# Query blocks of the differential heads from last to first, operands loaded by parts, and the gate's sigmoid by way of tanh

## The chip, the cores and the metric

The kernel runs on one core of one Trainium2 chip. The metric is device time in microseconds (us) of one execution. Five engines work side by side, each through its own instructions in order: TensorE (PE, matmuls and transposes; PEld is its weight load), VectorE (DVE), ScalarE (ACT), GpSimd (POOL) and SyncE (SP). SP does no arithmetic here; it issues most of the transfers (DMAs), POOL and ACT issue some. PSUM holds what matmuls write, in banks of 512 float32 a partition; SBUF holds the rest.

## The reference, cut to what matters

One decoder layer on 512 tokens of 2048 float32. A combined projection feeds four heads of gated linear attention (GLA) and four heads of differential softmax attention; their outputs side by side go through an output projection, and a gated MLP with a short convolution follows. The parts that the change touches:

```python
# differential attention, per head, causal, 4 blocks of 128 queries
s = einsum('bqhcd,bkhcd->bhcqk', qi, k) * scale + bias      # two score maps (c = 0, 1)
p = softmax(where(dist >= 0, s, -inf))
a = p[:, :, 0] - lam * p[:, :, 1]
o = einsum('bhqk,bkhe->bqhe', a, v)                          # then rmsnorm over the head
# gate of the GLA heads
gate = silu(gg)                                              # gg * sigmoid(gg)
o_a = rmsnorm(o_a, gla_norm) * gate
```

Query block qb sees keys 0 to 128 (qb + 1), so block 3 is four times as wide as block 0.

## The kernel before

Matrix products of the projections take float32 operands split in a high and a low part: `granule` (lines 128 to 140) copies a loaded `raw` tile with ACT into the high part (L137) and subtracts with DVE for the low part (L138), both into one of three slots of a tile called `ring`; three matmuls per pair of tiles then sum the products. `ring` is one tile of 7168 columns; the slots use at most its first 6896.

The token mixer's projection runs in ten units of 512 columns (`InUnit`, L727), each of which does seven block products instead of eight by sums of blocks (x0, z0, y0, z1, x1, y1, y2). Their weights are loaded with `load` (L102, on SP); some are added to a tile already there by POOL's accumulating DMAs (L751). Units 2, 3, 4 make the values and the operands of differential heads 0 and 1, units 5, 6, 7 those of heads 2 and 3, units 8 and 9 (`gate_unit`, L841) the gate. Results go to DRAM tiles (`dqd`, `dkd`: queries and keys of a head, already turned; `dvd`: values of two heads) and are fetched from there.

Beside the units runs a filler: the generators `gla_heads` and, after it, `diff_heads` (L617). `step` (L84) advances it, at a pace of 0.75 steps for each granule of a unit, 1.0 in the last unit. `diff_heads` is a pipeline over 16 blocks n (4 heads of 4 blocks). Step i calls, in this order, `store(i - 5)`, `values(i - 3)`, `probs(i)` and `turn(i - 2)`:

- `probs` (L637): two score maps (L645), bias, maximum, Exp (L653), sum, and the difference of the two maps;
- `turn` (L664): transposes of the block's probabilities, copied out by ACT as `aT` (L670);
- `values` (L673): the product of `aT` with the values (L677), then the norm, with its power on POOL;
- `store` (L686): two transposes (L690), a copy, and a DMA to `dstd` on ACT's queue (L693).

The queries and keys of a head fill four tiles of 128 x 512 under the tag `qk`, which has four buffers; the values fill one tile of 128 x 4 x 256 under the tag `v`, which has one. So the next head's queries and keys go where the last ones lay, and a load waits until these were read. `fetch(h + 1)` is called in the step of a head's last block, if the projection of head h + 1 is already traced (`there["diff"]`). Otherwise the next head's first step waits for it, fetches, and lets two more steps pass (two `yield`). `fetch_v(h)` is called in step 2 of head h, behind the `values` of the last block of head h - 1.

The gate (`done` in `gate_unit`) takes the unit's result u and the head's output op from DRAM: `op = op * u` (L850), `u = sigmoid(u)` on ACT (L851), `u = u * op` (L852). `turn_gate` (L870) and `place_diff` (L877) then lay the two groups' outputs out as the operand of the output projection.

Outside the blocks marked `manual_schedule`, where the written order holds, a planner orders the instructions of each engine: the order of tracing is the priority, and an instruction goes when a simulated timeline says that its operands and its buffer are ready. The differential heads and the gate are in the planned part. Dependences go by the part of a tile that is read or written.

Of the kernel before, what the change touches and what calls it, by code (L numbers as in the profile page):

```python
# [17 lines left out]
P = 128  # L18
D = 2048
S = 512  # L20
NT = S // P
# [4 lines left out]
DH, DQK, DDV = 4, 128, 256  # L26
# [9 lines left out]
def hybrid_layer(ctx: ExitStack, tc: tile.TileContext, x, attn_pre_norm, w_in, w_alpha_up, b_alpha,  # L36
# [10 lines left out]
    def dma(o, i):  # L47
        return nc.sync.dma_start(out=o, in_=i)
# [58 lines left out]
    RS = GR + P  # L107
    place_w = [LEVEL]

    ring = wpool.tile([P, 7 * GR], F32R, name="ring", bufs=1)  # L110
    slot = [0]

    def halves():
        slot[0] = (slot[0] + 1) % 3
# [218 lines left out]
    def qk_tile(name):  # L333
        return mx.tile([P, S], F32, name=name, tag="qk", bufs=4)
# [140 lines left out]
    there = {"gla": 0, "diff": 0}  # L475
# [141 lines left out]
    def diff_heads():  # L617
        dist = mx.tile([P, S], F32, name="dist", tag="md", bufs=1)
        nc.gpsimd.iota(dist, [[-1, S]], base=S - P, channel_multiplier=1, allow_small_or_imprecise_dtypes=True)
        nc.gpsimd.affine_select(dist, dist, [[-1, S]], ALU.is_ge, 1e34, base=S - P, channel_multiplier=1)  # L620
        dnb = mx.tile([P, DDV], F32, name="dnb", tag="nb", bufs=1)
        bcast_row(dnb, diff_norm[0])
        ts(dnb, dnb, 1.0 - LAMBDA_INIT, None, ALU.mult)
        qs, ks, vs = {}, {}, {}

        def fetch(h):
            qs[h], ks[h] = ([qk_tile(n) for _ in range(2)] for n in ("dq", "dk"))
            for i in range(2):
                dma(qs[h][i], dqd[h][:, i, :])
                dma(ks[h][i], dkd[h][:, i, :])  # L630

        def fetch_v(h):
            vs[h] = mx.tile([P, NT, DDV], F32, name="dvt", tag="v", bufs=1)
            e0 = (h % 2) * DDV
            dma(vs[h], dvd[h // 2][:, :, e0:e0 + DDV])

        def probs(n):  # L637
            h, qb = divmod(n, NT)
            q, k = qs[h], ks[h]
            slope = 2.0 ** (-8.0 * (h + 1) / DH)  # L640
            nk = (qb + 1) * P
            ps, ls = [], []
            for c in range(2):
                sb = bank()
                mm(sb[:, :nk], q[c][:, qb * P:(qb + 1) * P], k[c][:, :nk], start=True, stop=True)  # L645
# [7 lines left out]
                act(s[:, :nk], s[:, :nk], AF.Exp, bias=nm, scale=SC, accum_out=l)  # L653
# [7 lines left out]
            stt(ps[0][:, :nk], ps[0][:, :nk], ls[0], ps[1][:, :nk], ALU.mult, ALU.subtract)  # L661
            return ps[0]

        def turn(n, p):  # L664
            nk = (n % NT + 1) * P
# [4 lines left out]
            act(aT[:, :nk], tb[:, :nk], AF.Copy)  # L670
            return aT

        def values(n, aT):  # L673
            h, qb = divmod(n, NT)
            po = bank()
            for j in range(qb + 1):
                mm(po[:, :DDV], aT[:, j * P:(j + 1) * P], vs[h][:, j, :], start=j == 0, stop=j == qb)  # L677
            ss = small.tile([P, 1], F32, name="ss", tag="ss")
            jk = row_tile("jk")
            act(jk, po[:, :DDV], AF.Square, accum_out=ss)  # L680
            r = rsqrt_mean(ss, DDV)
            on = row_tile("on")
            stt(on, po[:, :DDV], r, dnb, ALU.mult, ALU.mult)
            return on

        def store(n, on):  # L686
            h, qb = divmod(n, NT)
            ob = bank(psm)
            for j in range(2):
                nc.tensor.transpose(ob[:, j * P:(j + 1) * P], on[:, j * P:(j + 1) * P], ident)  # L690
            o = row_tile("dst")
            act(o, ob[:, :2 * P], AF.Copy)
            nc.scalar.dma_start(out=dstd[h][:, :, qb * P:(qb + 1) * P], in_=o.rearrange("p (j c) -> p j c", j=2))  # L693

        N = DH * NT
        scored, turned, summed = {}, {}, {}
        fetch_v(0)
        for i in range(N + 5):
            h = i // NT
            if i < N and i % NT == 0:  # L700
                while there["diff"] <= h:
                    yield
# [138 lines left out]
    def gate_unit(c):  # L841
        heads = {}

        def before(j, i):
            op = heads[j, i] = tmp("op")
            dma(two(op), oad[2 * c + j][:, 2 * i:2 * i + 2, :])

        def done(j, i, u):
            op = heads.pop((j, i))
            tt(op, op, u, ALU.mult)  # L850
            act(u, u, AF.Sigmoid)  # L851
            tt(u, u, op, ALU.mult)  # L852
# [674 lines left out]
    u = ups[-1]  # L1527
# [161 lines left out]
```

## Time and profile before

| | |
|---|---|
| median of 3 runs | 2096.99 us (2095.53 to 2105.64) |
| profiled execution | 2102.56 us, its span 2100.9 us |
| PE busy | 2058.0 us, 98% of the span |
| DVE, ACT, POOL busy | 1504.4, 1001.0 and 286.3 us |
| HBM read and written | 311.72 and 44.56 MB, 170 GB/s over the span |
| differential heads on PE | first scores 386.28 us, last transposes 586.77 us |

The span runs from the first to the last recorded event; the execution's own time is 1.66 us longer. A row of the waits names an engine and line, what it waited for, then the total in us, the number of times and the longest. A row of the timeline has the start in us, the duration in us, the engine, the line, the operation, output and inputs, and in brackets the idle time before it with its releaser. A line number can be that of a helper: L48 is every plain DMA on SP, L102 every weight load.

### The profile page before, as it was taken

What the parts mean: (1) busy time and instruction counts of PE and PEld (TensorE: products, weight loads), DVE (VectorE), ACT (ScalarE), POOL (GpSimd) and SP (SyncE); (2) the same over time, 40 slices, a digit from 0 to 9 for tenths busy, and PEclk for the clock granted to TensorE, in tenths of its full rate; (3) what the DMA queues carried; (4) which work ended last, traced back from release to release, by engine and by line L of the source; (5) the groups of instructions that cost most, each with busy time, mean ns of one, the idle gap of its engine ahead of it and who ended that gap; (6) DMA issues with size and microseconds to landing.
All of it is one profiled execution on the core that took longest, in us unless ns stands there. A gap on an engine that the chain in (4) does not pass through costs nothing.

```text
span 2100.9 us, 35487 instructions
## 1 busy us (share of the span) xinstructions
PE 2058.0 (98%) x14417; PEld 1896.8 (90%) x14417; DVE 1504.4 (72%) x1790; ACT 1001.0 (48%) x1306; POOL 286.3 (14%) x306
## 2 busy tenths in 40 slices
PE   7999999999999999999999999999999999999997
PEld 6699999899988889899999999999999878887786
DVE  5967777666662255986777777777777778888877
ACT  5544444555652233454554554455455554444443
POOL 0112223222200000011111011111111110110100
PEclk9999999999999999999999999999999999999999
DMA  5488887878884244547668577567676876776763
GB/s 210 119 186 184 189 200 174 188 161 195 198 213 169 92 153 158 141 104 193 151 143 197 143 166 186 136 164 173 157 162 184 235 215 166 191 190 160 175 166 141
DMA packets 280698, 358.61 MB, mean 171 GB/s; under 512 B 14593, under 2 KB 221877, under 8 KB 278613
## 3 DMA queue, kind: packets, MB, share of 16 engines
q1 hardware_dynamic: 191380, 259.85, 36.9%
q0 software_dynamic: 84800, 94.38, 29.7%
q10 hardware_dynamic: 4352, 2.10, 0.4%
q8 instruction: 113, 1.85, 0.3%
q14 instruction: 53, 0.43, 0.1%
HBM read 311.72 MB, written 44.56 MB: 170 GB/s over the span
## 4 chain that ended last, share of the span: by engine, by line
PE 38%; issue 28%; DMA 2%; POOL 2%; DVE 1%; ACT 1%; POOLq 0%; DVEq 0%; SPq 0%; ACTq 0%
PE bank L1278 8%; PE bank L1279 8%; PE bank L1280 8%; PE bank L193 3%; PE bank L191 3%; PE bank L192 3%; POOL rt L1226 1%; PE bank L1381 1%; PE bank L1382 1%; POOL raw L1226 1%; PE bank L1380 1%; DMA raw<-in_w_ffn_in_dram 1%; DMA raw<-in_w_in_dram 1%; PE bank L1585 1%; PE bank L1586 1%
## 5 line engine op out<-in xcount | busy, mean ns | idle before, releaser
L138 DVE TENSOR_TENSOR ring<-raw,ring 128x1024 fp32r<-128x1024 f32 x315 | 383.5, 1223 | 277.9 <-ACT ring L137 277.1
L137 ACT ACTIVATE ring<-raw 128x1024 fp32r<-128x1024 f32 x315 | 333.3, 1060 | 520.9 <-PE bank L1279 112.4
L1280 PE MATMUL bank<-ah,ring 128*128 128x256 f32 x1280 | 353.4, 276 | 0.4 <-DVE ring L138 0.4
L1278 PE MATMUL bank<-ah,ring 128*128 128x256 f32 x1280 | 353.3, 276 | 0.0
L1279 PE MATMUL bank<-al,ring 128*128 128x256 f32 x1280 | 353.3, 276 | 0.0
L137 ACT ACTIVATE ring<-rt 128x1024 fp32r<-128x1024 f32 x221 | 233.1, 1060 | 241.2 <-PE bank L1279 147.9
L138 DVE TENSOR_TENSOR ring<-rt,ring 128x1024 fp32r<-128x1024 f32 x221 | 269.0, 1222 | 87.0 <-ACT ring L137 86.9
L1280 PEld LDWEIGHTS bank<-ah,ring 128*128 128x128 f32 x1280 | 240.3, 188 | 0.6 <-DVE ring L138 0.6
L1279 PEld LDWEIGHTS bank<-al,ring 128*128 128x128 f32 x1280 | 240.3, 188 | 0.1
L1278 PEld LDWEIGHTS bank<-ah,ring 128*128 128x128 f32 x1280 | 240.3, 188 | 0.1
L1381 PE MATMUL bank<-ring,ah 128*128 128x512 f32 x424 | 166.3, 392 | 5.3 <-DVE ring L138 5.3
L1382 PE MATMUL bank<-ring,al 128*128 128x512 f32 x424 | 165.2, 390 | 0.0
L1380 PE MATMUL bank<-ring,ah 128*128 128x512 f32 x424 | 158.8, 391 | 1.0 <-ACT ring L137 0.8
L192 PE MATMUL bank<-ring,ah 128*128 128x512 f32 x280 | 110.3, 395 | 0.9 <-DVE ring L138 0.9
L191 PE MATMUL bank<-ring,ah 128*128 128x512 f32 x280 | 109.9, 398 | 0.0
L193 PE MATMUL bank<-ring,al 128*128 128x512 f32 x280 | 109.7, 395 | 0.0
L1226 POOL DMA_DIRECT2D raw<-in_w_ffn_in_dram x40 | 51.2, 1308 | 398.1 <-DVE ring L138 398.1
L1381 PEld LDWEIGHTS bank<-ring,ah 128*128 128x128 f32 x424 | 79.6, 188 | 25.6 <-DVE ring L138 9.2
L1380 PEld LDWEIGHTS bank<-ring,ah 128*128 128x128 f32 x424 | 79.3, 188 | 19.9 <-ACT ring L137 3.4
L1226 POOL DMA_DIRECT2D rt<-in_w_ffn_in_dram x40 | 51.0, 1281 | 325.2 <-DVE ring L138 291.2
L777 PE MATMUL bank<-ring,ah 128*128 128x256 f32 x320 | 92.4, 289 | 2.6 <-ACT ring L137 1.3
L1382 PEld LDWEIGHTS bank<-ring,al 128*128 128x128 f32 x424 | 79.6, 188 | 16.3
(358 smaller groups left out, 5654.7 us busy)
## 6 DMA issues: line engine op xcount, KB each, us to landing
raw<-in_w_ffn_in_dram SPq DMA_DIRECT2D x96, 512.0 KB, 4.9
raw<-in_w_in_dram SPq DMA_DIRECT2D x56, 512.0 KB, 4.7
raw<-in_w_ffn_out_dram SPq DMA_DIRECT2D x48, 512.0 KB, 6.7
raw<-in_w_in_dram POOLq DMA_DIRECT2D x40, 512.0 KB, 7.1
rt<-in_w_ffn_in_dram SPq DMA_DIRECT2D x40, 512.0 KB, 5.7
rt<-in_w_ffn_in_dram POOLq DMA_DIRECT2D x40, 512.0 KB, 6.2
raw<-in_w_ffn_in_dram POOLq DMA_DIRECT2D x40, 512.0 KB, 6.8
raw<-in_w_o_dram SPq DMA_DIRECT2D x32, 512.0 KB, 4.0
```

Source lines behind the costliest of these rows:

```text
L137: act(hi, raw, AF.Copy)
L138: tt(lo, raw, hi.bitcast(F32), ALU.subtract)
L191: mm(banks[t], ah[:, t, s, :], w[0][:, k, :], start=st, stop=False)
L192: mm(banks[t], ah[:, t, s, :], w[1][:, k, :], start=False, stop=False)
L193: mm(banks[t], al[:, t, s, :], w[0][:, k, :], start=False, stop=sp)
L1226: nc.gpsimd.dma_start(out=raws[g].rearrange("p (a b) -> p a b", a=self.a), in_=self.block(0, j, g), accum_op=ALU.add)
L1278: mm(o, wh, sh[:, :, kk, :], start=start and kk == 0 and n == 0, stop=False, **NOW)
L1279: mm(o, wh, sl[:, :, kk, :], start=False, stop=False, **NOW)
L1280: mm(o, wl, sh[:, :, kk, :], start=False, stop=kk == HK - 1, **NOW)
L1380: mm(b[j], sh[:, o:o + P], w[0][:, q, :], start=start and st == 0, stop=False, **NOW)
L1381: mm(b[j], sh[:, o:o + P], w[1][:, q, :], start=False, stop=False, **NOW)
L1382: mm(b[j], sl[:, o:o + P], w[0][:, q, :], start=False, stop=st == 3, **NOW)
```

## The change

Three things are done.

Block n of head h is now block 3 - n of its queries (`place_of`), so each head begins with its widest block and ends with its narrowest.

Queries, keys and values of all heads use tiles that are made once. `fetch(h, lo, hi)` loads columns 128 lo to 128 hi of the four tiles. Behind the scores of block r = 2 the columns 256 to 511 of head h + 1 are fetched, if its projection is traced by then, and behind r = 3 the rest. Otherwise the head is fetched whole at its first step, which then lets three steps pass instead of two. The values are loaded in four parts, two of them in step 1 and two in step 2 of each head, behind the `values` of that step (all four at the start for head 0); part 0 of an odd head goes to 256 columns at the end of `ring` that no slot uses.

The gate uses sigmoid(u) = (1 + tanh(u / 2)) / 2: 0.5 op u, then tanh(0.5 u), then (tanh + 1) times the product.

```diff
     ring = wpool.tile([P, 7 * GR], F32R, name="ring", bufs=1)
+    ring_end = ring[:, 6 * RS:6 * RS + 256].bitcast(F32)
...
-        qs, ks, vs = {}, {}, {}
-        def fetch(h):
-            qs[h], ks[h] = ([qk_tile(n) for _ in range(2)] for n in ("dq", "dk"))
+        q, k = ([qk_tile(n) for _ in range(2)] for n in ("dq", "dk"))
+        vt = mx.tile([P, NT, DDV], F32, name="dvt", tag="v", bufs=1)
+
+        def value_tile(h, j):
+            return ring_end if j == 0 and h % 2 else vt[:, j, :]
+
+        def fetch(h, lo, hi):
+            sl = slice(lo * P, hi * P)
             for i in range(2):
-                dma(qs[h][i], dqd[h][:, i, :])
-                dma(ks[h][i], dkd[h][:, i, :])
-        def fetch_v(h):
-            vs[h] = mx.tile([P, NT, DDV], F32, name="dvt", tag="v", bufs=1)
+                dma(q[i][:, sl], dqd[h][:, i, sl])
+                dma(k[i][:, sl], dkd[h][:, i, sl])
+
+        def fetch_v(h, *js):
             e0 = (h % 2) * DDV
-            dma(vs[h], dvd[h // 2][:, :, e0:e0 + DDV])
+            for j in js:
+                dma(value_tile(h, j), dvd[h // 2][:, j, e0:e0 + DDV])
+
+        def place_of(n):
+            h, r = divmod(n, NT)
+            return h, NT - 1 - r
...
-        fetch_v(0)
+        got = set()
+
+        def ahead(h, r):
+            if r == 2 and h + 1 < there["diff"]:
+                fetch(h + 1, 2, 4)
+                got.add(h + 1)
+            elif r == 3 and h + 1 in got:
+                fetch(h + 1, 0, 2)
+
+        fetch_v(0, 3, 2, 1, 0)
...
-                if h not in qs:
-                    fetch(h)
+                if h not in got:
+                    fetch(h, 0, 4)
+                    got.add(h)
+                    yield
                     yield
                     yield
...
             if i - 3 in turned:
                 summed[i - 3] = values(i - 3, turned.pop(i - 3))
-            if i % NT == 2 and i > NT and h < DH:
-                fetch_v(h)
+                if i % NT == 1 and h < DH:
+                    fetch_v(h, 3, 2)
+                elif i % NT == 2 and h < DH:
+                    fetch_v(h, 1, 0)
             if i < N:
                 scored[i] = probs(i)
-                if i % NT == 3 and h + 1 < there["diff"]:
-                    fetch(h + 1)
+                ahead(h, i % NT)
...
-            tt(op, op, u, ALU.mult)
-            act(u, u, AF.Sigmoid)
-            tt(u, u, op, ALU.mult)
+            stt(op, op, 0.5, u, ALU.mult, ALU.mult)
+            act(u, u, AF.Tanh, scale=0.5)
+            stt(u, u, 1.0, op, ALU.add, ALU.mult)
```

More of the change, by code (lines that the diff above doesn't have):

```diff
@@ L623, in diff_heads @@
         ts(dnb, dnb, 1.0 - LAMBDA_INIT, None, ALU.mult)
-        qs, ks, vs = {}, {}, {}
-        def fetch(h):
-            qs[h], ks[h] = ([qk_tile(n) for _ in range(2)] for n in ("dq", "dk"))
+        q, k = ([qk_tile(n) for _ in range(2)] for n in ("dq", "dk"))
[4 more added lines that the diff above has]
+            sl = slice(lo * P, hi * P)
             for i in range(2):
-                dma(qs[h][i], dqd[h][:, i, :])
-                dma(ks[h][i], dkd[h][:, i, :])
-        def fetch_v(h):
-            vs[h] = mx.tile([P, NT, DDV], F32, name="dvt", tag="v", bufs=1)
+                dma(q[i][:, sl], dqd[h][:, i, sl])
+                dma(k[i][:, sl], dkd[h][:, i, sl])
+        def fetch_v(h, *js):
             e0 = (h % 2) * DDV
-            dma(vs[h], dvd[h // 2][:, :, e0:e0 + DDV])
+            for j in js:
[3 more added lines that the diff above has]
+            return h, NT - 1 - r
         def probs(n):
-            h, qb = divmod(n, NT)
-            q, k = qs[h], ks[h]
+            h, qb = place_of(n)
             slope = 2.0 ** (-8.0 * (h + 1) / DH)
@@ L664, in turn @@
         def turn(n, p):
-            nk = (n % NT + 1) * P
+            nk = (place_of(n)[1] + 1) * P
             tb = bank()
@@ L673, in values @@
         def values(n, aT):
-            h, qb = divmod(n, NT)
+            h, qb = place_of(n)
             po = bank()
             for j in range(qb + 1):
-                mm(po[:, :DDV], aT[:, j * P:(j + 1) * P], vs[h][:, j, :], start=j == 0, stop=j == qb)
+                mm(po[:, :DDV], aT[:, j * P:(j + 1) * P], value_tile(h, j), start=j == 0, stop=j == qb)
             ss = small.tile([P, 1], F32, name="ss", tag="ss")
@@ L686, in store @@
         def store(n, on):
-            h, qb = divmod(n, NT)
+            h, qb = place_of(n)
             ob = bank(psm)
```

## The prediction

> **What bounds the kernel now.** I read the page first, then the stretch that the edit touches: the differential heads and the two gate units, 367 to 660 us.
>
> ```profile
> span 2100.9 us, 35487 instructions
> PE 2058.0 (98%) x14417; PEld 1896.8 (90%) x14417; DVE 1504.4 (72%) x1790; ACT 1001.0 (48%) x1306; POOL 286.3 (14%) x306
> ```
>
> TensorE (PE) is busy for 98% of the span. The edit adds and removes no matmul, so what it can give is idle time of PE. The next view cuts the stretch into windows (length, busy time of PE, PEld, DVE, ACT and POOL, granted clock, DMA share, GB/s).
>
> ```profile
> 367.00:420.00 53.00, 49.74 (x383) 47.42 (x383) 34.87 (x76) 26.91 (x55) 11.18 (x14) 0.97 0.80 187
> ...
> 525.00:551.00 26.00, 24.49 (x197) 23.87 (x196) 14.97 (x26) 14.01 (x23) 5.10 (x6) 1.00 1.02 230
> ...
> 577.00:603.00 26.00, 24.64 (x206) 24.03 (x204) 11.27 (x13) 11.99 (x19) 5.36 (x7) 1.00 0.99 228
> 603.00:630.00 27.00, 24.11 (x154) 21.46 (x155) 22.45 (x31) 16.21 (x26) 0.00 (x0) 1.00 0.63 192
> ```
>
> PE idles 3.26, 1.51, 1.36 and 2.89 us in these four. The waits of PE between 330 and 660 us say for whom (total, times, longest):
>
> ```profile
> PE bank L645 <- DMA dk<-dkd: 3.3, 1, 3.3
> PE bank L677 <- ACT aT L670: 1.8, 2, 1.5
> PE bank L777 <- ACT ring L137: 1.3, 1, 1.3
> PE bank L777 <- ACT ah L150: 1.2, 1, 1.2
> PE bank L864 <- DVE p L852: 0.9, 1, 0.9
> PE bank L677 <- DMA dvt<-dvd: 0.9, 1, 0.9
> PE bank L779 <- DVE ring L138: 0.8, 1, 0.8
> ...
> ```
>
> Together 10.2 us, 0.5% of the run. The longest has a second price, which the windows around it show:
>
> ```profile
> 408.00:411.40 3.40, 0.17 (x2) 0.00 (x0) 0.79 (x4) 0.68 (x2) 0.74 (x2) 0.91 1.12 317
> 411.40:413.00 1.60, 1.57 (x7) 1.60 (x8) 0.73 (x4) 0.00 (x0) 0.00 (x0) 0.50 1.08 386
> 413.00:415.00 2.00, 2.00 (x15) 2.00 (x14) 0.51 (x3) 1.27 (x2) 0.00 (x0) 0.69 0.73 258
> ```
>
> After the idle 3.26 us the granted clock is 0.50, then 0.69: 1.6 x 0.50 + 2.0 x 0.31 = 1.4 us of lost work. The 1.5 us gap in the window from 525 leaves the clock at 1.00. So the edit has at most 10.2 + 1.4 = 11.6 us to win here.
>
> **The change, part by part.** All sums are made against the profiled execution (2102.56 us, 1.7 us of it around the span), which is 5.6 us above the median of the runs, 2096.99; I take the difference over to the median.
>
> *Operands of the next head.* Before, `fetch(h + 1)` stands behind the scores of a head's last block (r = 3) and loads four whole 256 KB tiles. After, columns 256 to 511 go out behind r = 2, the rest behind r = 3, if the next head's projection is there by r = 2. That is so for head 1 only: heads 2 and 3 are fetched whole as before, 18 us ahead of use (472.43 and 491.04 below, for head 2) and without a wait of PE. SP and PE around head 1's fetch, in order of time:
>
> ```profile
> 400.61 1.88 PE L645 MATMUL bank<-dk,dq 128*128 128x512 f32 x4
> 402.29 0.37 SPq L48 DMA_DIRECT2D dvd<-u  x1
> 402.75 0.50 SPq L48 DMA_DIRECT2D dq<-dqd  x1
> 403.30 1.07 SPq L48 DMA_DIRECT2D dk<-dkd  x1
> ...
> 405.32 1.02 PE L677 MATMUL bank<-dvt,aT 128*128 128x256 f32 x4
> ...
> 411.43 0.77 PE L645 MATMUL bank<-dk,dq 128*128 128x128 f32 x2 [3.26 <-DMA dk<-dkd]
> ...
> 424.94 1.89 PE L677 MATMUL bank<-dvt,aT 128*128 128x256 f32 x8
> ...
> 472.43 0.34 SPq L48 DMA_DIRECT2D dq<-dqd  x1
> ...
> 491.04 0.61 PE L645 MATMUL bank<-dk,dq 128*128 128x128 f32 x4
> ```
>
> The first k tile, issued at 403.30, lands at about 411.4; PE came for it at 411.43 - 3.26 = 408.17. After, the second halves cannot go out much earlier, since the store of 402.29 stands ahead of them on SP. Two things help. First, 256 KB less (half of q, half of k) stand in front: at the 240 GB/s or so that the stretch moves (230 in the 525 row, 317 in the 408 row) that is about 1.1 us. Second, PE has more to do before it comes: `values(1)` now has six matmuls instead of four (1.02 to about 1.45 us, between the rows of four and eight) and `turn(1)` one transpose more, 0.5 us. So about 1.6 us of the wait go, and with a gap of 1.6 us left the clock should hold, as after 525: another 1.4 us. **Term: -3.0 us.** Bounds: -4.7 (wait and clock loss gone) and 0 (the load lands as before). I take a value in between because the landing times are queue more than size:
>
> ```profile
> DMA to landing us min/median/max: 6.9/7.4/8.0
> DMA to landing us min/median/max: 6.6/6.6/6.6
> ```
>
> The first row is the 256 KB dk loads, the second the 512 KB dvt loads: twice the bytes, no later. Here the Trainium skill speaks against the edit ("DMA: Bandwidth & Descriptors", section on the anatomy of one DMA): about 2 us of fixed cost per transfer and the bytes at 436 GB/s on top. By it a half tile lands only 0.3 us sooner, and the term would be -0.8 us instead of -3.0, since the gap would stay long enough to lower the clock. The two rows lean its way as to size; that is the first rival.
>
> *Values by parts.* One load of 512 KB a head becomes four of 128 KB. Before, it must wait for the last block of the head before (the eight matmuls at 424.94, done 426.8):
>
> ```profile
> 426.86 0.58 SPq L48 DMA_DIRECT2D dvt<-dvd  x1
> ...
> 433.56 0.67 PE L677 MATMUL bank<-dvt,aT 128*128 128x256 f32 x2 [0.86 <-DMA dvt<-dvd]
> SPq L48 <- PE bank L677: 10.2, 3, 5.8
> ```
>
> From last block to first, part 3 is free after the first block, part 2 after the second, and so on; part 0 of odd heads goes to the unused end of the ring, so no part waits for the last block. The parts can go out a step earlier, a step being some 7.6 us, from the scores at 400.61 to those due at 408.17. The wait goes. **Term: -0.9 us**, bounds -0.9 and 0.
>
> *More transfers on SP.* Twelve more for values, four more for head 1's halves: 16 at 0.3 to 0.6 us of SP's time (rows above), some 7 us over 200 us. SP idles between them, which hides it. Behind them stand the weight loads of the units; of the gaps in PE, only 1.3 us are put down to a split that waits for such a load, so these loads have a lead. **Term: +0.3 us**, bounds 0 and +2 (four in a row ahead of one weight load).
>
> *A third `yield`* moves heads 0, 2 and 3 one step later. PE has unit matmuls to fill it. At the end:
>
> ```profile
> 586.77 0.38 PE L690 MATMUL bank<-ident,on 128*128 128x128 f32 x2
> ...
> 604.17 7.56 SPq L48 DMA_DIRECT2D dt<-dstd  x4
> ```
>
> A step of 7.6 us puts the last store's transposes near 594, still 10 us ahead of the reload. **Zero**; bounds 0 and +2, if that lead is used up.
>
> *Order of the blocks.* The sums of matmuls, softmax and transposes are the same; only large and small blocks change place. **Zero**, bounds -1 and +1.
>
> *Sigmoid by Tanh.* Now Sigmoid and Exp take the function table from each other:
>
> ```profile
> L851 ACT ACT_TABLE_LOAD  x3: 1283/1283/1283, 539.0 to 575.9; - x3
> L653 ACT ACT_TABLE_LOAD  x2: 1283/1283/1283, 547.9 to 559.5; - x2
> L850 DVE TENSOR_TENSOR op<-op,u x6: 687/691/693, 535.4 to 620.7; 128x512 f32<-128x512 f32 x6
> L661 DVE SCALAR_TENSOR_TENSOR s<-s,rl x16: 341/547/748, 395.6 to 575.8; 128x128 f32<-128x128 f32 x4, 128x256 f32<-128x256 f32 x4, 128x384 f32<-128x384 f32 x4, 128x512 f32<-128x512 f32 x4
> 542.29 1.06 ACT L137 ACTIVATE ring<-raw 128x1024 fp32r<-128x1024 f32 x1 [1.35 <-DMA raw<-in_w_in_dram]
> 545.97 0.63 ACT L851 ACTIVATE p<-p 128x512 f32<-128x512 f32 x1 [1.04 <-DVE op L850]
> 547.03 1.56 PE L677 MATMUL bank<-dvt,aT 128*128 128x256 f32 x6 [1.51 <-ACT aT L670]
> ```
>
> Up to 5 x 1.28 = 6.4 us of ACT go; none, if Tanh needs a table of its own. The Trainium skill ("ScalarE: Activation LUTs", section on table sets) lists tanh in the set of exp, so all five should go; no row here shows a Tanh. ACT is half idle, and PE's one long wait for it, at 547.03, comes down a chain that begins with a weight load (542.29), then a split, a product and the Sigmoid at 545.97, ahead of the copy that PE needs; no table load stands in it. DVE gets 16 `scalar_tensor_tensor` for `tensor_tensor`, at most 748 - 691 = 57 ns each, 0.9 us in all, on an engine idle for a third of the stretch. **Zero**, bounds -1.5 and +0.9.
>
> *The end of the stretch.* The waits of 1.3, 1.2, 0.9 and 0.8 us are after 601 us, behind weight loads issued into DMA queues that are full (share 0.99). No byte is taken away there. **Zero**, bounds -2 and +2.
>
> Sum: -3.0 - 0.9 + 0.3 = **-3.6 us**, so 2099.0 in an execution like the profiled one and **2093.4 us** at the median.
>
> **The rivals.**
> 1. *The halves land as late as the whole* (landing set by queue and fixed cost). For: the two landing rows. Against: 256 KB fewer are ahead in the same queue. The dk term shrinks to the 0.5 us of added PE work; -0.5 - 0.9 + 0.3 = -1.1: 2095.9 us.
> 2. *SP is held by the value loads: slower.* SP works in order. The row quoted above shows its head held 10.2 us by value matmuls in three places. After, each head has two pairs that wait for earlier blocks; a held pair delays the weight load behind it, and the splits and PE behind that. For: that row, and DMA shares of 1.02 and 0.99 where heads 3 and the gates meet, so that a late load isn't caught up. Against: parts are free earlier than the whole was. It decides from the point where a hold exceeds the lead of the weight loads. Price: the 10.2 us reach PE in place of SP, -3.6 + 10.2 = +6.6: 2103.6 us.
> 3. *Nearly all waits go*, as a lighter ACT and a shorter last block let the copies and splits run ahead too: -4.7 - 0.9 - 1.8 - half of the 4.2 after 601 = -9.5: 2087.5 us. For: three of these waits are on ACT. Against: the chains shown begin with DMA.
>
> That the halves aren't reached (projection too late at r = 2) would not cost: head 1 would then be fetched three steps ahead, as heads 2 and 3 are.
>
> **How the numbers follow.** Forecast 0.45, first rival 0.25, second 0.17, third 0.13. The likeliest is 2093.4. The shown runs of one kernel spread from 2095.53 to 2105.64, so a median has an uncertainty of some 3 us. The range goes from the third rival's neighbourhood, 2086, to the second's, 2104; the unknown terms (+2 on SP, +2 for the yield, +2 at the end) fit in it. The forecast's own range is 2089 to 2098. What a measurement can tell from no change is about 0.5%, 10.5 us: 2086.5 and 2107.5. Faster than that needs the third rival and some luck: 0.11. Slower needs the second with a clock loss on top: 0.06. Within: 0.83.
>
> **What would show it.** Right: PE waits for dk near 411 us under 2 us with a clock of 1.00 behind it; no PE wait for the value loads; SP issues for dq and dk of head 1 in two groups; no table load from 530 to 640 us; DVE's gate products below 0.75 us; the waits after 601 still there. Wrong: a clock of 0.50 in the stretch again; new PE waits for splits whose raw loads were issued right behind value loads; a PE wait for the gate's products that grew; or a difference that arises after 660 us, where the edit has nothing.

## The result, and the profile after

The changed kernel takes 2089.38 us at the median of six runs (2083.65 to 2090.44). The kernel before, run beside it, takes 2100.31 us (2095.53 to 2106.15). The ratio is 0.9941, 95% interval 0.9919 to 0.9963: faster by 0.6%, and the interval holds the 0.5% that the prediction took as the limit of what can be told. Profiled execution against profiled execution it is 2090.44 against 2102.56 us, 12.1 us less, where the steps of the prediction came to 3.6.

The page of the changed kernel begins:

```profile
span 2088.7 us, 35508 instructions
PE 2053.1 (98%) x14417; PEld 1893.3 (91%) x14417; DVE 1502.4 (72%) x1790; ACT 993.8 (48%) x1301; POOL 290.4 (14%) x306
```

PE runs the same 14417 matmuls; five instructions are gone from ACT (1306 before). So the place of the 12.1 us has to be found by stretches. Two events on ACT bracket the differential heads and the gate in every kernel here: the load of the function table for Exp and that for Gelu. Before, then after, from the timeline of ACT:

```profile
134.40 1.28 ACT L567 ACT_TABLE_LOAD   x1
...
843.98 1.28 ACT L1119 ACT_TABLE_LOAD   x1 [2.96 <-DVE u L1118]
```

```profile
131.75 1.28 ACT L568 ACT_TABLE_LOAD   x1
...
829.22 1.28 ACT L1139 ACT_TABLE_LOAD   x1 [2.96 <-DVE u L1138]
```

From one to the other it is 709.58 us before and 697.47 after: **the stretch is 12.1 us shorter, as much as the whole**. Ahead of it these two profiles differ by 2.7 us (134.40 to 131.75) and behind it by 2.6 the other way (1256.9 to 1259.5); second profiles of the same kernels, below, put the start at 132.97 and 132.35 and the part behind at 1256.9 and 1257.2, so neither repeats. The stretch is also the finest measure to be had: what lies behind it varied by 3 us over the kernels below without relation to their edits. The windows of exactly this stretch (sum of the lengths, busy time by engine), before and after:

```profile
sum 709.58, PE 698.50 PEld 654.11 DVE 434.83 ACT 324.46 POOL 118.02; mean PE 698.50 PEld 654.11 DVE 434.83 ACT 324.46 POOL 118.02
```

```profile
sum 697.47, PE 694.52 PEld 651.59 DVE 433.26 ACT 317.80 POOL 120.45; mean PE 694.52 PEld 651.59 DVE 433.26 ACT 317.80 POOL 120.45
```

PE's idle time went from 709.58 - 698.50 = 11.1 us to 2.95 us, and its busy time from 698.5 to 694.5. The waits of PE in the core of the stretch (330 to 660 us) say what is left of the eight rows of before:

```profile
PE bank L797 <- ACT ah L151: 1.9, 1, 1.9
PE bank L676 <- DVE s L669: 0.3, 1, 0.3
```

L797 is L777 of before, L676 is L668. The waits for dk, for the values, for aT, and for the splits in the ring are gone. The windows that answer to those of the prediction:

```profile
367.00:420.00 53.00, 52.72 (x402) 49.03 (x401) 36.53 (x73) 27.26 (x53) 13.37 (x15) 1.00 0.83 194
...
525.00:551.00 26.00, 26.00 (x198) 23.96 (x198) 19.56 (x33) 12.32 (x24) 4.49 (x6) 1.00 0.99 222
...
577.00:603.00 26.00, 24.09 (x201) 23.51 (x200) 19.32 (x26) 14.54 (x23) 1.92 (x2) 1.00 0.79 231
603.00:630.00 27.00, 27.00 (x127) 22.49 (x126) 13.22 (x16) 10.57 (x15) 0.00 (x0) 1.00 0.82 297
```

The clock, 0.97 in the first window before, is 1.00. Cut into windows of 2 us, before loses 1.7 us between 330 and 660 us to a lower clock (the sum of each length times one minus its granted clock), after nothing. So idle time gives 8.1 us and the clock 1.7; the other 2.3 us are a shorter busy time of PE at full clock, which no row puts down to anything.

### The profile page after: what moved, and what is told of

Read it like the earlier page. It is cut to its first block, busy times and chain, and to the rows that moved or that the text cites. A ratio compares the mean times of both kernels' runs of the same rounds, so it can differ in the third digit from the quotient of the medians.

```text
span 2088.7 us, 35508 instructions
## 1 busy us (share of the span) xinstructions
PE 2053.1 (98%) x14417; PEld 1893.3 (91%) x14417; DVE 1502.4 (72%) x1790; ACT 993.8 (48%) x1301; POOL 290.4 (14%) x306
## 4 chain that ended last, share of the span: by engine, by line
PE 61%; issue 28%; DMA 4%; DVE 3%; POOL 2%; ACT 1%; POOLq 0%; DVEq 0%; SPq 0%; ACTq 0%
PE bank L1300 8%; PE bank L1299 7%; PE bank L1298 7%; PE bank L192 3%; PE bank L193 3%; PE bank L194 3%; PE bank L793 3%; PE bank L795 3%; PE bank L794 3%; PE bank L797 3%; PE bank L798 2%; PE bank L799 2%; PE bank L176 1%; PE bank L174 1%; PE bank L175 1%
## 5 line engine op out<-in xcount | busy, mean ns | idle before, releaser
L797 PE MATMUL bank<-ring,ah 128*128 128x256 f32 x320 | 92.0, 288 | 1.9 <-ACT ah L151 1.9
```

The lines of the kernel that those rows point to most:

```text
L797: mm(o, sh[:, n, kk, :], wh[:, k, :], start=st, stop=False, **NOW)
```

## The experiments

Two accounts of the gain stood against each other: that the parts of operands and values brought it, as the prediction's terms have it, or that the order of the blocks, the third step and the missing table loads did, all three priced at nothing there. Each kernel below was profiled once, and its stretch was taken apart in the same way. "Rest" is the stretch without idle time and clock loss; the clock loss is summed over windows of 2 us from 330 to some 650 us; the ratio is against the kernel before on the same chip (none where it was run only for its profile).

| kernel | stretch us | PE idle | clock loss | rest | ratio, 95% interval |
|---|---|---|---|---|---|
| before | 709.58 | 11.1 | 1.7 | 696.8 | |
| before, again | 710.92 | 9.8 | 5.1 | 696.0 | |
| before with Tanh | 706.76 | 8.6 | 1.7 | 696.4 | 0.9987 (0.9974 to 1.0) |
| before with the order | 704.49 | 7.2 | 0 | 697.3 | 0.9979 (0.9966 to 0.9993) |
| before with order and Tanh | 702.06 | 5.8 | 0 | 696.3 | 0.9966 (0.9953 to 0.9979) |
| before without the fetch ahead | 703.16 | 6.7 | 0 | 696.4 | 0.998 (0.997 to 0.999) |
| before, simple version | 702.31 | 4.9 | 1.7 | 695.7 | 0.9965 (0.9949 to 0.9981) |
| after | 697.47 | 3.0 | 0 | 694.5 | 0.9941 (0.9919 to 0.9963) |
| after, again | 698.02 | 3.2 | 0 | 694.8 | |
| after with Sigmoid | 702.34 | 4.3 | 1.7 | 696.3 | 0.9971 (0.9957 to 0.9985) |
| after with table loads | 702.70 | 4.6 | 3.4 | 694.7 | 0.996 (0.9946 to 0.9974) |
| after, operands whole | 699.01 | 3.5 | 0 | 695.5 | 0.9947 (0.9927 to 0.9967) |
| after, values whole | 696.89 | 2.2 | 0 | 694.6 | 0.995 (0.9934 to 0.9966) |
| after, two steps | 699.68 | 3.9 | 0 | 695.8 | 0.9959 (0.9945 to 0.9973) |

The clock loss comes in lumps of 1.7 us, and the rest moves over 2.8 us without an order that the edits explain; so a stretch is read together with its idle time, and a difference of 1.5 us in it decides nothing alone.

**The kernels as they were, profiled again.**

```diff
 (no line of either kernel changed)
```

> The kernel before once more, to see how far the stretch from the Exp to the Gelu table load moves from one profiled execution to the next: within 1 us of 709.6 if the stretch is a measure good for the differences read so far; 3 us away if it isn't.

> The changed kernel once more, for the same reason: within 1 us of 697.5 if the stretch is a good measure, 3 us away if it isn't.

The stretch came out at 710.92 and 698.02 us, 1.3 and 0.6 us from the first profiles, the former just outside the 1 us expected. Before, the idle time was 1.3 us less and the clock took 3.4 us more. The difference of the two kernels is 12.9 us this time: it is that of the kernels, not of one profile.

**Tanh alone, and all but Tanh.** My theory after the result was that the table loads have a price end to end; the rival, the prediction's own step, that ACT's idle time hides them.

```diff
 # in the kernel before (in the changed kernel: the other way round)
-            tt(op, op, u, ALU.mult)
-            act(u, u, AF.Sigmoid)
-            tt(u, u, op, ALU.mult)
+            stt(op, op, 0.5, u, ALU.mult, ALU.mult)
+            act(u, u, AF.Tanh, scale=0.5)
+            stt(u, u, 1.0, op, ALU.add, ALU.mult)
```

> The kernel before with only the gate by Tanh; all it computes stays. Theory 1 (the gain is the head operands' waits): the five table loads go, the stretch from the Exp table load near 134 us to the Gelu table load near 844 us (709.6 us before, 697.5 after the whole change) stays within 1.5 us of 709.6, and the 3.3 us wait for dk with its clock loss stays; ratio 0.999 to 1.001. Theory 2 (ACT's 6.4 us of table loads stood behind the waits for aT and those after 601 us): the stretch shortens by 5 to 7 us, the waits after 601 us go, ratio about 0.997.

> The changed kernel with Sigmoid put back in the gate. Theory 1: the stretch from the Exp to the Gelu table load stays near 697.5 us (within 1.5), ratio to before about 0.994. Theory 2: five table loads come back, the waits for aT and after 590 us with them, and the stretch grows by 5 to 7 us to about 703; ratio about 0.997. Theory 3 (any edit re-plans the stretch and the waits fall by chance): the stretch lands anywhere between 697 and 710, in no relation to the part undone.

Tanh alone takes 2.8 us off the stretch, 2.4 of them idle time of PE: between the two expectations, at most 1.5 and 5 to 7. Sigmoid put back into the changed kernel adds 4.9 us: 1.4 of idle time, one lump of the clock, 1.8 of the rest. Their ratios (0.9987; 0.9971 against 0.9941) say the same, the first just at the edge of no change. What remained of PE's waits in the kernel before with Tanh, and in the changed kernel with Sigmoid:

```profile
PE bank L645 <- DMA dk<-dkd: 3.1, 1, 3.1
PE bank L677 <- ACT aT L670: 1.3, 1, 1.3
...
```

```profile
PE bank L797 <- ACT ring L138: 0.8, 1, 0.8
PE bank L799 <- DVE ring L139: 0.7, 1, 0.7
...
PE bank L685 <- ACT aT L678: 0.6, 1, 0.6
...
```

In the first, the row for the ring's copy (L137, 1.3 us before) is missing and dk stays; in the second, waits for the ring's copy and split and for aT are back, and dk is not. That points to the copies that stand behind the loads on ACT.

The two pairs tell more. With Sigmoid and with Tanh, PE, ACT, DVE and POOL each do the same instructions in the same order through the first 480 us of the stretch, to behind the gate, and the gate's own last as long (medians: ACT's function 625 to 632 ns, DVE's products 682 to 694). So another order by the planner is no rival here, and the kernels of a pair can be compared instruction by instruction, each counted from the start of its stretch. The kernel before is level with its Tanh version on PE up to 541 us (0.1 us behind), 1.2 us behind from 576, past its five loads, 2.5 behind at 605, past the ring copy that takes the last accumulating weight load, and 2.8 from 612 on. In the changed pair, the kernel with Sigmoid is 2.3 us behind at 559, 2.5 at 591, and 4.9 from 603 on, past the same copy and a lump of the clock. Not all of this is the loads': its ring copy at 531.34 waits for a weight load that landed 1.6 us later than in the changed kernel, and that is ahead of its first table load, at 532.41. So the loads cost 2.8 us in the kernel before, and at most 4.9 in the changed one.

**The loads or the arithmetic?** Sigmoid differs from Tanh in its products too, so the table loads alone were put into the changed kernel:

```diff
             stt(op, op, 0.5, u, ALU.mult, ALU.mult)
+            sg = small.tile([P, 1], F32, name="nm", tag="nm")
+            act(sg, u[:, :1], AF.Sigmoid)
             act(u, u, AF.Tanh, scale=0.5)
```

The result of this Sigmoid, of one column, is not used.

> The changed kernel with a Sigmoid of one column, whose result isn't used, ahead of each Tanh of the gate. It brings the table loads back (about five of 1.28 us) with the gate's arithmetic left as it is, and adds eight ACT instructions of some 0.2 us. If the loads on ACT are what Sigmoid costs, the stretch from the Exp to the Gelu table load is 701 to 704 us, near the 702.3 of the kernel with Sigmoid, and the last accumulating weight load is issued and lands later against the PE work than in the changed kernel (issued 577.00, ACT took it at 585.77); ratio 0.996 to 0.998. If the cost is in another order that the planner gave the Sigmoid kernel by chance, the stretch stays at 697 to 699 us, ratio 0.994 to 0.995.

The five loads are there again, between 530 and 567 us, and the stretch is 702.70 us, that of the changed kernel with Sigmoid (702.34): 1.6 us more idle time than the changed kernel, and two lumps of the clock. By itself this run would leave a rival: the ratio's interval overlaps that of the changed kernel, and here the planner did move instructions (on POOL, the power of a norm now stands ahead of the second of the four loads shown next, in the changed kernel behind it). Together with the pairs, where no instruction moved, it is the loads. How they reach PE is seen best at the end of the gate units, where POOL issues four accumulating loads and ACT takes the last of them into the ring. The first and the last of the four, and that copy, in the kernel before, before with Tanh, the changed kernel, and the changed kernel with the loads:

```profile
575.59 1.29 POOL L751 DMA_DIRECT2D wt<-in_w_in_dram  x1 [3.80 <-DVE ring L138]
...
586.31 1.32 POOL L751 DMA_DIRECT2D raw<-in_w_in_dram  x1 [2.08 <-DVE ring L138]
...
601.37 1.06 ACT L137 ACTIVATE ring<-raw 128x1024 fp32r<-128x1024 f32 x1 [4.84 <-DMA raw<-in_w_in_dram]
```

```profile
582.61 1.32 POOL L751 DMA_DIRECT2D raw<-in_w_in_dram  x1 [2.10 <-DVE ring L138]
...
596.27 1.06 ACT L137 ACTIVATE ring<-raw 128x1024 fp32r<-128x1024 f32 x1 [3.50 <-DMA raw<-in_w_in_dram]
```

```profile
562.92 1.30 POOL L771 DMA_DIRECT2D wt<-in_w_in_dram  x1 [2.63 <-DVE ring L139]
...
577.00 1.32 POOL L771 DMA_DIRECT2D raw<-in_w_in_dram  x1 [0.36 <-issue]
...
585.77 1.06 ACT L138 ACTIVATE ring<-raw 128x1024 fp32r<-128x1024 f32 x1 [2.00 <-DMA raw<-in_w_in_dram]
```

```profile
566.04 1.30 POOL L771 DMA_DIRECT2D wt<-in_w_in_dram  x1 [3.65 <-DVE ring L139]
...
576.03 1.30 POOL L771 DMA_DIRECT2D raw<-in_w_in_dram  x1 [0.36 <-issue]
...
593.14 1.06 ACT L138 ACTIVATE ring<-raw 128x1024 fp32r<-128x1024 f32 x1 [4.22 <-DMA raw<-in_w_in_dram]
594.25 0.58 PE L797 MATMUL bank<-ring,ah 128*128 128x256 f32 x1 [2.71 <-ACT ring L138]
```

(Before with Tanh, only the last.) Between the kernel before and its Tanh version, the last load is issued 1.2 us later, as counted from the start of the stretch, and is taken into the ring 15.1 us after its issue instead of 13.7: 2.6 us later in all. In the changed kernel with the loads, the first goes out at 566.04, 1.9 us later than in the changed kernel, and so do the two behind it (1.7 to 3.3 us); then the four stand close together, and the last is taken 17.1 us after its issue, against 8.8. PE waits 2.71 us for it. That the last load itself is issued later, as I had it in mind, is wrong here: it is issued 2.2 us sooner by the same count. Why it lands so much later stays open. Closeness is not the whole of it: with Sigmoid the four go out over 13.9 us, as in the changed kernel (14.1), and the last is taken 12.4 us after its issue; with two steps instead of three, below, without a table load, they go out over 9.2 us, the last is taken 13.2 us later, and PE waits 0.2 us for a split.

**The order of the blocks alone, then with Tanh.**

```diff
 # in the kernel before
+        def place_of(n):
+            h, r = divmod(n, NT)
+            return h, NT - 1 - r
...
-            h, qb = divmod(n, NT)          # probs, values, store
+            h, qb = place_of(n)
-            nk = (n % NT + 1) * P          # turn
+            nk = (place_of(n)[1] + 1) * P
```

> The kernel before with only the order of the query blocks turned round; whole fetches, one load of values, Sigmoid. Theory 1: the whole operands of head 1 are still fetched behind its last scores, so the wait for dk stays at 2 to 3.5 us and the clock drops behind it; the values are still late; the stretch is 708 to 711 us, ratio 0.999 to 1.001. Rival (the order alone does it, since the narrow blocks at a head's end free SP, ACT and DVE earlier): dk wait under 1 us, the stretch at 700 to 704, ratio about 0.996.

> The kernel before with two parts of the change: blocks from last to first, and the gate by Tanh; whole fetches, one load of values, two steps of waiting. If the two parts act on separate waits, their gains in the stretch from the Exp to the Gelu table load add: 709.6 - 5.1 - 2.8 = 701.7 us, ratio about 0.9966; the remaining 4.2 us to the changed kernel's 697.5 are then due to the loads by parts or the third step. If the planner merely re-deals the waits, the stretch is nearer 697.5 or above 704.

The order, priced at nothing in the prediction, takes 5.1 us off the stretch with the operands still loaded whole, next to the rival's range of 700 to 704; with Tanh it is 7.5 us, the sum of the two edits (5.1 + 2.8 = 7.9) within what repeats differ by. The timeline of SP and PE in the kernel with the order alone shows what it does to head 1's operands, and what it does to the values:

```profile
407.18 0.45 SPq L48 DMA_DIRECT2D dk<-dkd  x1
...
413.92 1.10 PE L649 MATMUL bank<-dk,dq 128*128 128x512 f32 x2 [1.14 <-DMA dk<-dkd]
...
500.90 1.37 SPq L48 DMA_DIRECT2D dvt<-dvd  x1
...
508.61 1.97 PE L681 MATMUL bank<-dvt,aT 128*128 128x256 f32 x8 [2.14 <-ACT s L664]
```

The first k tile has 412.78 - 407.18 = 5.6 us from issue to need (before: 408.17 - 403.30 = 4.9) and takes 6.7 us instead of 8.1. The wait is 1.1 us instead of 3.3, and the clock, which lost 1.7 us there, stays at 1.00. But the widest block now comes first for the values too: head 2's whole load is issued at 500.90 and the eight matmuls wait 2.14 us at 508.61. The row names ACT's s, which is not what these matmuls read; the profile has this load land 7.6 us after its issue, at 508.5, while the copy of aT that they read ended at 506.4. So it is the load that comes late.

**Head 1's operands whole, in the changed kernel; and no fetch ahead, in the kernel before.**

```diff
 # in the changed kernel
-            if r == 2 and h + 1 < there["diff"]:
-                fetch(h + 1, 2, 4)
+            if r == 3 and h + 1 < there["diff"]:
+                fetch(h + 1, 0, 4)
                 got.add(h + 1)
-            elif r == 3 and h + 1 in got:
-                fetch(h + 1, 0, 2)
 # in the kernel before
                 scored[i] = probs(i)
-                if i % NT == 3 and h + 1 < there["diff"]:
-                    fetch(h + 1)
```

> The changed kernel with head 1's queries and keys fetched whole behind its last scores instead of in halves. Theory 1: the wait for dk comes back at 2 to 3.3 us with 1.4 us of clock loss; the stretch is 700.5 to 702.5 us, ratio about 0.996. Rival (landing is queue and fixed cost, the halves are no earlier, and what removes the wait is the changed order of PE's work): the stretch stays within 1 us of 697.5, no wait for dk over 1 us, ratio about 0.994.

> The kernel before without fetching a head's operands behind the scores of the last block of the head before; head 1 is then fetched at its own first step, two steps ahead of use, as heads 2 and 3 are. It measures the price of the wait for dk by itself. Theory: the 3.3 us wait and the 1.4 us of low clock go and PE's other work fills the two steps: stretch 704 to 706 us, ratio about 0.998. Rival: the later heads push the gate's waits out, and the gain is given back after 540 us: stretch 708 to 711, ratio 0.999 to 1.001.

With whole tiles the changed kernel has a stretch of 699.01 us, 1.0 to 1.5 more than with halves (between the two expectations), and no wait for dk. Its timeline, and that of the changed kernel with halves:

```profile
408.84 0.42 SPq L48 DMA_DIRECT2D dk<-dkd  x1
...
414.23 1.10 PE L653 MATMUL bank<-dk,dq 128*128 128x512 f32 x2
```

```profile
396.92 0.42 SPq L48 DMA_DIRECT2D dk<-dkd  x1
...
408.38 0.42 SPq L48 DMA_DIRECT2D dk<-dkd  x1
...
412.81 1.02 PE L653 MATMUL bank<-dk,dq 128*128 128x512 f32 x2
```

The whole tile is issued at 408.84 and read at 414.23 without a wait, so it landed in under 5.4 us; of the halves the second goes out at 408.38 and has 412.81 - 408.38 = 4.4 us, enough too. Two things set these times apart. One is the distance from POOL's transfers. In each kernel POOL issues two accumulating loads of 512 KB ahead of the fetch; the second of them, before, with the order alone, and in the changed kernel with whole tiles:

```profile
401.63 1.27 POOL L751 DMA_DIRECT2D raw<-in_w_in_dram  x1 [0.40 <-DVE rl L655]
```

```profile
402.06 1.27 POOL L755 DMA_DIRECT2D raw<-in_w_in_dram  x1 [1.23 <-DVE rl L659]
```

```profile
400.76 1.27 POOL L769 DMA_DIRECT2D raw<-in_w_in_dram  x1 [1.11 <-DVE rl L663]
```

From there to the issue of the first k tile (403.30, 407.18, 408.84) it is 1.7, 5.1 and 8.1 us, and the tile is there 8.1, 6.7 and under 5.4 us after its issue: the farther behind, the sooner it lands. No run changes this distance alone (the two weight loads that stand behind the fetch on SP before stand ahead of it in the other two), so the accumulating loads are the likely cause, not a shown one.

The other is size. The q tiles of head 1, issued between 400 and 415 us in the changed kernel and in the one with whole tiles (how many, KB each, median us to landing):

```profile
dq<-dqd SPq DMA_DIRECT2D x2, 128.0 KB, 3.8
```

```profile
dq<-dqd SPq DMA_DIRECT2D x2, 256.0 KB, 5.4
```

That is 1.6 us for half the bytes. For the first k tile it is 1.1: the half lands in 5.6 us where it is issued 5.6 us behind POOL's load (two steps instead of three, below), the whole in 6.7 us at 5.1 us behind (order alone). So the prediction's 1.1 us for 256 KB less in front was a fair price. The rule of the Trainium skill that it set against it ("DMA: Bandwidth & Descriptors", anatomy of one DMA), by which half a tile saves 0.3 us, is given there for transfers that GpSimd issues, while these are SP's; the measurement decides. But with the order and the third step the fetch is far enough behind that the whole tile is in time too. The other edit, without any fetch ahead, takes head 1's operands at its own first step and lets two steps pass. It gives 6.4 us of the stretch from two lines that are left out: the wait for dk is gone, and the clock stays at 1.00 there (703.16 us, a little below the 704 to 706 expected).

**The values whole, in the changed kernel.**

```diff
-            return ring_end if j == 0 and h % 2 else vt[:, j, :]
+            return vt[:, j, :]
...
-        def fetch_v(h, *js):
+        def fetch_v(h):
             e0 = (h % 2) * DDV
-            for j in js:
-                dma(value_tile(h, j), dvd[h // 2][:, j, e0:e0 + DDV])
+            dma(vt, dvd[h // 2][:, :, e0:e0 + DDV])
...
-                if i % NT == 1 and h < DH:
-                    fetch_v(h, 3, 2)
-                elif i % NT == 2 and h < DH:
-                    fetch_v(h, 1, 0)
+                if i % NT == 2 and h < DH:
+                    fetch_v(h)
```

> The changed kernel with each head's values loaded whole, in one transfer behind the last block of the head before (no part in the ring's end). Theory: only the wait for dvt comes back, 0.3 to 0.9 us; stretch 697.5 to 699 us, ratio 0.994 to 0.995. Rival: the early parts are what removes the rest of the waits, since the whole load holds SP in front of the weight loads; stretch near 701.5, ratio about 0.996.

The stretch is 696.89 us, and the ratio 0.995; the wait for values that was expected is not there: the parts are worth nothing that can be measured in this kernel. At head 2, where the kernel with the order alone waited 2.14 us, the timeline has:

```profile
501.71 0.57 SPq L48 DMA_DIRECT2D dvt<-dvd  x1
...
508.59 1.89 PE L684 MATMUL bank<-dvt,aT 128*128 128x256 f32 x8
```

508.59 - 501.71 = 6.9 us from issue to use are enough here, and 508.61 - 2.14 - 500.90 = 5.6 us were too few there, where it took 7.6.

**Two steps instead of three, in the changed kernel.**

```diff
                     got.add(h)
                     yield
                     yield
-                    yield
```

> The changed kernel with two steps instead of three between a head's fetch and its first scores. Theory: nothing hangs on the third step, as no head that is fetched whole waited for its operands with two; stretch 697 to 699 us, ratio about 0.994. Rival: the third step moves head 0's and 1's work off the weight loads, and without it the waits near 410 us and after 590 us come back; stretch 700 to 702, ratio about 0.996.

The stretch is 2.2 us longer than the first profile of the changed kernel and 1.7 longer than the second; the idle time is 0.8 to 1.0 us more. Of it one row is new:

```profile
PE bank L653 <- DMA dk<-dkd: 0.8, 1, 0.8
```

The third step, priced at nothing, moved heads 0, 2 and 3, and by it all that comes before head 1's fetch: that goes out 8.1 us behind POOL's second load with three steps, 5.6 with two. The intervals of the two ratios overlap, so what is shown of the step's worth is this row.

**A simple version**: the kernel before with the order, Tanh, no fetch ahead and three steps, without parts.

```diff
                     fetch(h)
                     yield
                     yield
+                    yield
...
-                if i % NT == 3 and h + 1 < there["diff"]:
-                    fetch(h + 1)
 (and the order and Tanh as above)
```

> The kernel before with four small edits: blocks from last to first, Tanh in the gate, no fetch of a head behind the last scores of the head before, and three steps instead of two between a head's fetch and its first scores. No halves, no values by parts, no tiles that last. If nothing of the gain hangs on loads by parts, the stretch from the Exp to the Gelu table load is 695 to 699 us and the ratio 0.994 to 0.9955, as with the changed kernel. If the loads by parts carry the 4.6 us that reversal and Tanh left (702.06 against 697.47), the stretch is 700.5 to 703 and the ratio about 0.9965; a wait for the values of head 2 of about 2 us near 508 us would then be seen again.

It was to show whether the parts are needed at all: 702.31 us and 0.9965, as expected if they are, no better than order and Tanh alone. One row says why:

```profile
PE bank L681 <- DMA dvt<-dvd: 2.5, 1, 2.5
...
```

It is head 3's values this time, at 561 us, with a lump of clock loss behind it. So parts of the values are worth nothing in the kernel as it fell out; where a head's first block comes close behind its whole load, they would have 2 to 4 us to save, which no run here tries. No version beat the changed kernel beyond what runs differ by.

## Why the prediction was right and where it was wrong

The time of 2089.38 us lies in the range, 4.0 us below the forecast of 2093.4 and nearest to the third rival (2087.5). That is in part luck. As a gain it is 10.9 us (2100.31 to 2089.38) against a forecast of 3.6, three times as much; the forecast was counted from 2096.99 us, 3.3 us below the median of the kernel before that was measured beside the change, and the range of 18 us was wide enough. By the ratio the gain is 0.6% with the 0.5% bound inside its interval, so the runs don't tell "within" from "faster", and 0.83 against 0.11 was too sure. The third rival, at a chance of 0.13, fits best in its reasons too: it put 9.5 us on the waits and the clock, 9.8 were measured, and it named a lighter ACT, which the runs with Tanh bear out, and shorter last blocks, whose order did count, if mainly by way of head 1's fetch. Step by step:

**What bounds the kernel** held. The forecast put 11.6 us at stake, idle time and clock; 9.8 of the 12.1 us came from there.

**Operands of the next head**, -3.0: the sign was right, the size -4.7 (its own bound; 5.0 with the clock loss as measured by windows of 2 us). Of its reasons, the 256 KB fewer in front are worth about the 1.1 us that it gave them, but were not needed: with whole tiles the wait is gone too. What the step left out is the order, which alone shortens the wait from 3.3 to 1.1 us and saves the clock, and the third step, without which 0.8 us of it stay even with halves. Both put the fetch farther behind POOL's accumulating loads, and the farther, the sooner it landed. The first rival, that the halves land as late as the whole, did not come true.

**Values by parts**, -0.9: that wait is gone, but also with the load whole. What the step missed is that reversing the order makes the first block the widest, so a whole load that was early enough for the two matmuls of block 0 can be late for the eight of block 3 (2.1 to 2.5 us in three kernels, order alone, order with Tanh, and the simple version). The parts would cover the order's own risk.

**More transfers on SP**, +0.3, and the second rival: SP is held longer than before. Its waits, 330 to 660 us, in the changed kernel:

```profile
SPq L48 <- PE bank L685: 18.3, 7, 4.5
...
SPq L48 <- PE bank L653: 13.4, 4, 7.5
```

Value matmuls hold its head for 18.3 us in place of 10.2, and those of the scores for 13.4, yet no weight load behind them keeps PE waiting: PE has no wait for a split left in the changed kernel. The rival asked the right question; the lead of the weight loads outlasted these holds, the longest of 7.5 us.

**The third step** and **the order**, both zero: these fell. The order alone is worth 5.1 us of the stretch, the third step some 2 (0.8 to 1.0 of it idle time). The zero of the order rested on the sums of work being the same, that of the step on PE having other work. But a fetch races with the blocks between its issue and its use; the order's bounds (±1) had no row behind them.

**Sigmoid by Tanh**, zero: this fell most clearly. What the Trainium skill says ("ScalarE: Activation LUTs", section on table sets), that tanh is in exp's set, the trace bears out: no table load stands between 131.75 and 829.22 us in the changed kernel. The gate's products did not grow (medians 682 to 694 ns with either function; the 57 ns were a needless fear). The failed step is the sentence that ACT is half idle and no load stands in the chain of its one long wait. That chain was one of several: the five loads put ACT, which works in order, behind by up to 3.2 us, with it the copies that PE and the accumulating loads wait for, and the last of these reaches PE late, behind 601 us. They cost 2.8 us alone, and at most 4.9 within the change; how the late landing comes about is open.

**The end of the stretch**, zero since no byte is taken away: fell too. Of 4.2 us of waits 1.9 are left (2.7 with Tanh alone, 3.0 with the order alone), and the last accumulating load is taken 8.8 instead of 15.1 us after its issue.

**The clock** after a gap of 1.5 us "should hold": no rule, see below. The marks that were named held but one: no wait for dk or for values, a clock of 1.00, two groups of issues for head 1, no table load, DVE's products under 0.75 us. The waits after 601 us were to stay, and half of them went.

## What to carry to other kernels

A step that leaves all sums of work the same, an order or a step more of distance, isn't free: write down for each load what lies between its issue and its use, and who else is in the queues then. On an engine that takes its work in order, idle time in the mean does not hide all: a function table that changes five times cost 2.8 us here for 6.4 us of loads, and at most 4.9 in the changed kernel, by way of the copies behind them. And a load by parts is worth its lines only where the whole one is shown to be late.

## What was not expected of the hardware

The granted clock does not fall by the size of a gap, but by what PE does in fixed windows. The traces record when it changed, and between any two changes lies a whole multiple of 3.413 us. Cut there: the changed kernel with Sigmoid, then the kernel before, then the same kernel profiled again:

```profile
592.46:595.88 3.42, 1.88 (x14) 1.47 (x13) 2.21 (x3) 2.49 (x3) 0.00 (x0) 1.00 0.29 108
595.88:599.29 3.41, 3.41 (x18) 3.41 (x18) 3.41 (x5) 1.58 (x2) 0.00 (x0) 0.50 0.76 231
```

```profile
598.55:601.97 3.42, 2.59 (x23) 2.39 (x21) 0.00 (x0) 0.60 (x1) 0.00 (x0) 1.00 0.68 222
601.97:605.38 3.41, 2.15 (x16) 1.94 (x17) 2.89 (x4) 2.22 (x4) 0.00 (x0) 1.00 0.10 24
605.38:608.79 3.41, 2.51 (x23) 2.31 (x23) 3.10 (x4) 1.52 (x3) 0.00 (x0) 1.00 0.67 208
```

```profile
600.26:603.67 3.41, 1.27 (x10) 0.87 (x8) 1.37 (x2) 2.46 (x3) 0.00 (x0) 1.00 0.17 62
603.67:607.08 3.41, 3.41 (x16) 3.41 (x17) 3.38 (x5) 1.61 (x3) 0.00 (x0) 0.50 0.61 179
```

1.5 us idle in one window lowered the clock in the first; 0.8 and 1.3 us in two neighbouring windows did not in the second; 2.1 us in one window did in the third. Of all such windows at full clock between 330 and 660 us, in the fourteen profiles, the seven in which PE was busy for 55% or less were followed by one at half clock, and none with 56% or more was. (It is no exact rule elsewhere: a window of 74%, at 63 us before, was followed by half clock, and one of 52%, at 1688 us with the order alone, was not.) Each window at half clock costs 1.7 us, the lump of the table. Where the windows lie against the start of the span differs from run to run, so the same gap can end either way. The Trainium skill ("TensorE: Matmul & The Clock Gate", Part 1) has the clock at a half or whole, decided over free-running windows of 3.4 us: the traces agree. Its advice (section "Why this matters for your kernels"), no idle gap over about 3 us, is too mild by these rows. So a gap of 1.5 us or more, ahead of a run, is priced as its length plus a chance of 1.7 us.
